# Differential attention on one core: two-bank score tiles, one softmax maximum per component, normalisation moved to the output

## The chip, the core and the metric

The kernel runs on one core of one Trainium2 chip. It is one program for a whole inference step. The metric is the device time of one execution in microseconds (us). Each engine (PE = TensorE, with its weight loads as PEld; DVE = VectorE; ACT = ScalarE; POOL = GpSimd; SP, which here only issues DMAs) works through its own list of instructions in a fixed order and waits at an instruction until its operands and its output buffer are ready.

## The reference, cut to what matters

The step has two layers. The second one's mixer is differential attention, for a prompt of 1024 tokens and for 8 sample sequences of 8 tokens. The change touches the prompt part, and one buffer of the sample part.

```
def diff_attend(q, q_pos, kv, k_pos, lam):            # 8 heads, 2 components of 64, values of 128
    s = einsum('bthcd,bshcd->bhcts', q * 64**-0.5, k)
    s = where(k_pos <= q_pos, s, NEG)
    a = softmax(s, axis=-1)
    w = a[:, :, 0] - lam * a[:, :, 1]
    return einsum('bhts,bshe->bthe', w, v)
def diff_out(o, ...):                                 # rms_norm over the 128 values of a head, then w_out
    return (rms_norm(o, subnorm) * (1 - lam_init)).reshape(B, T, -1) @ w_out
```

Each head has two score matrices (components). Each is softmaxed by itself, the second is subtracted with the factor lam, and the difference multiplies the values.

## The kernel before, in words

**Tiling.** The prompt's attention is cut into 64 units: 8 heads by 8 blocks of 128 queries. Unit (h, i) looks at the w = (i+1)*128 keys up to its own block. Units with i < 4 (w up to 512) are called short, the others long.

**A unit has two parts.** `scores(h, i)`, lines 1235 to 1275: for each component and for each stretch of up to 512 keys ("bank") PE computes the scores into a PSUM tile `S` of one bank (three of them, `SB`). DVE takes the negated row maximum (L1254), ACT takes exp with this maximum and sums the row (L1255) into the SBUF tile `P` (four of 128x1024, `PB`). A long unit has two banks per component with a maximum each, so DVE and ACT then bring the two to a common maximum with small operations on `ml` (L1259 to L1263, ACT's in L1261). DVE takes the reciprocals of the two sums (L1264) and multiplies them by 1 and -lam (L1265; for long units also L1267). POOL scales component 0 (L1271) and DVE adds component 1 times its factor (L1272), one bank at a time. `values(h, i)`, lines 1277 to 1297: PE transposes the weights in groups of four blocks into a PSUM tile `tr`, ACT copies them to `WT`, and PE multiplies them by V into a PSUM tile `av` of its own pool (two of them, `AVB`, shared with the sample's). DVE copies `av` to the output (L1294) and ACT sums its squares (L1296).

**PSUM.** There are 8 banks: three `S`, three `tr` (`TRB`), two `av`. The tile `tr` also serves the transposes of the sample's cached keys (`kt`, evicted to `KT` by DVE L99 and ACT L97 in turn), of the next head's keys and queries (`kn`, read by ACT and DVE in `qk_prep`), the sample's scores (`Qz`, L1388) and the transposes of a finished head (`fin`, L1300 to L1311).

**What sets the order.** The pieces of all units are Python generators. `stagger` merges them by a table of start times and durations: units of a head in the order 7, 0, 6, 1, 5, 2, 4, 3, each `values` behind its `scores` by `PLAG`, the sample's work spread over the same time. A list scheduler then fixes every engine's order when the program is built: it goes by that order and by its own estimate of when operands and buffers come free. Nothing is reordered on the chip.

**What follows.** `out_proj` (L770 to L815) multiplies the heads' outputs `oT` by w_out. It first splits them into two parts: `oh` by ACT (L97) and the rest by DVE and POOL (L104). Its first matmuls are `dn`. Head 7's `fin` runs inside it, on the PSUM tile `up`.

Of the kernel before, what the change touches and what calls it, by code (L numbers as in the profile page):

```python
# [12 lines left out]
AF = mybir.ActivationFunctionType  # L13
# [11 lines left out]
TRB, SB, AVB, KTB, KTT, VTB, VLAG, WTB, PLAG, PB, SEND = 3, 3, 2, 6, 4, 4, 5, 4, 6, 4, 0.92  # L25
# [46 lines left out]
class Step:  # L72
# [1114 lines left out]
    def diff_prompt(self, oT):  # L1187
# [3 lines left out]
        fac = kp("fac", [128, 2])  # L1191
# [10 lines left out]
        def begin():  # L1202
            self.diff_lambda(kp, sp)
            nc.vector.memset(fac[:, 0:1], 1.0)
            nc.vector.tensor_copy(fac[:, 1:2], self.nlam)
            yield
# [29 lines left out]
        def scores(h, i):  # L1236
# [4 lines left out]
            ml = sp("ml", [128, 14], bufs=3)  # L1241
            nm, l = (ml[:, x:x + 4].rearrange("p (n c) -> p n c", c=2) for x in (0, 4))
            banks = [(b0, min(w, b0 + 512)) for b0 in range(0, w, 512)]
            P = []
            for c in range(2):
                P.append(sp("P", [128, 1024], bufs=PB))
                for n, (b0, b1) in enumerate(banks):
                    S = pp("S", [128, 512], bufs=SB)
                    o = S[:, 0:b1 - b0]
                    self.mm(o, X[c][:, qs], A[c][:, b0:b1], True, False)  # L1250
                    self.mm(o, X[c][:, qs], B[c][:, b0:b1], False, b1 < w)
                    if b1 == w:
                        self.mm(S[:, w - 128 - b0:w - b0], self.identb, self.masks[:, 0, :], False, True)
                    nc.vector.tensor_reduce(nm[:, n, c:c + 1], o, AX.X, OP.max, negate=True)  # L1254
                    nc.scalar.activation(P[c][:, b0:b1], o, AF.Exp, bias=nm[:, n, c:c + 1], accum_out=l[:, n, c:c + 1])  # L1255
                    yield
            if len(banks) == 2:
                m, e = ml[:, 8:10], ml[:, 10:14].rearrange("p (n c) -> p n c", c=2)
                nc.vector.tensor_tensor(m, nm[:, 0], nm[:, 1], OP.min)  # L1259
                nc.vector.tensor_tensor(e, m.unsqueeze(1).to_broadcast([128, 2, 2]), nm, OP.subtract)  # L1260
                nc.scalar.activation(e, e, AF.Exp)  # L1261
                nc.vector.tensor_tensor(l, l, e, OP.mult)
                nc.vector.tensor_tensor(l[:, 0], l[:, 0], l[:, 1], OP.add)  # L1263
            nc.vector.reciprocal(l[:, 0], l[:, 0])  # L1264
            nc.vector.tensor_tensor(l[:, 0], l[:, 0], fac, OP.mult)  # L1265
            if len(banks) == 2:
                nc.vector.tensor_tensor(e, e, l[:, 0:1].to_broadcast([128, 2, 2]), OP.mult)  # L1267
            else:
                e = l
            for n, (b0, b1) in enumerate(banks):  # L1270
                nc.gpsimd.tensor_scalar(P[0][:, b0:b1], P[0][:, b0:b1], e[:, n, 0:1], 0.0, op0=OP.mult, op1=OP.add)  # L1271
                nc.vector.scalar_tensor_tensor(P[0][:, b0:b1], P[1][:, b0:b1], e[:, n, 1:2], P[0][:, b0:b1],  # L1272
                                               op0=OP.mult, op1=OP.add)
            st[h, i] = P[0]
            yield

        def values(h, i):
            V, ssq = st[h][3:]
            W = st[h, i]
# [9 lines left out]
            av = pp("av", [128, 128], bufs=AVB)  # L1289
# [4 lines left out]
            nc.vector.tensor_copy(oT[h][:, i * 128:i * 128 + 128], av)  # L1294
            sq = sp("sq", [128, 128], bufs=2)
            nc.scalar.activation(sq, av, AF.Square, accum_out=ssq[:, i:i + 1])  # L1296
# [21 lines left out]
        for h in range(8):  # L1318
            if h < 7:
                gens.append((t + 2, 40, 8, prep(h + 1)))  # L1320
            for i in (7, 0, 6, 1, 5, 2, 4, 3):
                gens.append((t, i + 2, 3 if i < 4 else 5, scores(h, i)))
# [302 lines left out]
```

## Time and profile before

| | us |
|---|---|
| median of 3 runs (3436.47 to 3440.07) | 3436.64 |
| the profiled execution, its own time | 3439.05 |
| its span, first to last instruction | 3437.3 |
| second attention and its end, 2131 to 2556 of the span | 425 |
| of these, 2131 to 2500 / 2500 to 2556 | 369 / 56 |

Times within the span count from its first instruction. Busy times of engines overlap. A wait is put down to what came last. The stretch from 2131 us, where the in-projection has ended on PE, to 2556 us, where `out_proj` runs steadily, holds nearly all that the change touches: the rest of the program is the first layer before it, and the second MLP behind it. The sample's attention runs all through the stretch to about 2512 us, beside the prompt's.

### The profile page before, as it was taken

The numbers are of one execution on the slowest core, as the hardware profiler recorded it, in microseconds if no ns is written. First come the engines' busy times: TensorE is split into PE (matmuls) and PEld (weight loads), VectorE is DVE, ScalarE is ACT, GpSimd is POOL, SyncE is SP. The second block draws the span as 40 slices with busy tenths as digits, with TensorE's granted clock in tenths as the row PEclk, the third lists the DMA queues.
The fourth block names the chain that finished last, engine by engine and source line by source line (L and its number), as shares of the span: only waits on it lengthen the run. The fifth ranks groups of instructions, "written<-read, shape, count | busy, mean of one in ns | idle before, by whom it ended". The sixth has DMA issues, their size and how long they took to land.

```text
span 3437.3 us, 59207 instructions
## 1 busy us (share of the span) xinstructions
PE 3325.9 (97%) x22990; PEld 2879.1 (84%) x22990; DVE 1907.2 (55%) x4043; ACT 1199.5 (35%) x2912; POOL 748.2 (22%) x1034
## 2 busy tenths in 40 slices
PE   8989989999999999999999999999979999999998
PEld 7779768787789999999997877777769899999998
DVE  5345666667655544444447224888764554444545
ACT  5222466666642111111114122777743111111111
POOL 1232235545421100011005113222220110011102
PEclk9999999999999999999999999999989999999999
DMA  7233510000022111111104223677522111111111
GB/s 251 77 102 112 151 56 14 18 21 2 1 84 68 50 44 33 48 50 50 44 32 157 74 77 120 200 231 240 191 84 75 43 48 45 31 50 50 50 31 53
DMA packets 243083, 271.01 MB, mean 79 GB/s; under 512 B 28626, under 2 KB 191602, under 8 KB 242674
## 3 DMA queue, kind: packets, MB, share of 16 engines
q1 hardware_dynamic: 242802, 267.23, 24.6%
q8 instruction: 181, 2.97, 0.4%
q14 instruction: 100, 0.82, 0.1%
HBM read 229.81 MB, written 41.50 MB: 79 GB/s over the span
## 4 chain that ended last, share of the span: by engine, by line
PE 63%; DVE 5%; ACT 3%; issue 0%; DMA 0%; POOL 0%; SPq 0%; DVEq 0%; ACTq 0%; POOLq 0%
PE dn L107 27%; PE up L107 22%; PE ps L107 8%; PE tr L110 2%; PE av L107 2%; PE S L107 1%; ACT P L1255 1%; DVE P L1272 1%; DVE ml L1254 1%; PE tr L1388 1%; DVE oT L104 1%; DVE hl L260 0%; DVE KT L99 0%; DVE xT L1088 0%; ACT WT L97 0%
## 5 line engine op out<-in xcount | busy, mean ns | idle before, releaser
L1088 DVE TENSOR_TENSOR xT<-xT,dn 128x512 f32<-128x512 f32 (+2 forms) x768 | 404.2, 530 | 497.3 <-PE dn L107 496.4
L107 PE MATMUL dn<-xh,dh 128*128 128x512 f32 (+2 forms) x1536 | 504.5, 328 | 0.7 <-DVE xT L1088 0.7
L107 PE MATMUL up<-hh,uh 128*128 128x512 f32 (+2 forms) x1536 | 503.9, 328 | 1.2 <-DVE u L1064 1.2
L107 PE MATMUL dn<-xl,dh 128*128 128x512 f32 (+2 forms) x1536 | 504.6, 329 | 0.0
L107 PE MATMUL dn<-xh,dl 128*128 128x512 f32 (+2 forms) x1536 | 503.4, 328 | 0.0
L107 PE MATMUL up<-hh,ul 128*128 128x512 f32 (+2 forms) x1536 | 502.8, 327 | 0.0
L107 PE MATMUL up<-hl,uh 128*128 128x512 f32 (+2 forms) x1536 | 502.4, 327 | 0.0
L100 POOL TENSOR_SCALAR xh<-u 128x512 fp32r<-128x512 f32 (+2 forms) x192 | 142.8, 744 | 1309.5 <-PE dn L107 858.6
L1065 ACT ACTIVATE u<-u 128x512 f32<-128x512 f32 (+2 forms) x192 | 96.4, 502 | 829.4 <-DVE u L1064 827.4
L107 PEld LDWEIGHTS up<-hh,uh 128*128 128x128 f32 x1536 | 289.7, 189 | 25.1 <-DVE u L1064 1.8
L107 PEld LDWEIGHTS up<-hl,uh 128*128 128x128 f32 x1536 | 289.7, 189 | 22.3
L107 PEld LDWEIGHTS up<-hh,ul 128*128 128x128 f32 x1536 | 289.6, 189 | 22.3
L107 PEld LDWEIGHTS dn<-xh,dh 128*128 128x128 f32 x1536 | 289.5, 189 | 21.5 <-DVE xT L1088 1.1
L107 PEld LDWEIGHTS dn<-xh,dl 128*128 128x128 f32 x1536 | 289.2, 188 | 21.6
L107 PEld LDWEIGHTS dn<-xl,dh 128*128 128x128 f32 x1536 | 289.4, 188 | 19.8
L721 POOL TENSOR_SCALAR P<-P,ml,gates 128x64 f32<-128x64 f32 (+8 forms) x384 | 244.7, 653 | 257.2 <-DVE ml L718 205.5
L107 PE MATMUL ps<-wh,hh 128*128 128x512 f32 (+2 forms) x720 | 277.2, 386 | 3.7 <-ACT hh L97 2.7
L107 PE MATMUL ps<-wh,hl 128*128 128x512 f32 (+2 forms) x720 | 277.3, 385 | 0.7 <-DVE hl L104 0.4
L107 PE MATMUL ps<-wl,hh 128*128 128x512 f32 (+2 forms) x720 | 277.2, 385 | 0.1
L107 PE MATMUL S<-A,X 128*128 128x512 f32 (+7 forms) x608 | 252.8, 416 | 23.3 <-ACT P L1255 11.1
L110 PE MATMUL tr<-ident,P 128*128 128x128 f32 (+1 forms) x1584 | 240.8, 281 | 17.9 <-DVE P L1272 10.6
L714 ACT ACTIVATE P<-S,ml 128x64 f32<-128x64 f32 (+8 forms) x384 | 216.6, 572 | 101.3 <-DVE ml L711 66.0
(334 smaller groups left out, 6423.8 us busy)
## 6 DMA issues: line engine op xcount, KB each, us to landing
ur<-in_mlp_w_up_dram SPq DMA_DIRECT2D x64, 512.0 KB
dr<-in_mlp_w_down_dram SPq DMA_DIRECT2D x64, 512.0 KB
kt<-in_cache_diff_kv_dram SPq DMA_DIRECT2D x64, 512.0 KB
vt<-in_cache_diff_kv_dram SPq DMA_DIRECT2D x64, 512.0 KB
xT<-x_saved SPq DMA_DIRECT2D x16, 544.0 KB
zq<-ro SPq DMA_DIRECT2D x32, 256.0 KB
kv<-in_cache_nsa_sel_dram SPq DMA_DIRECT2D x64, 128.0 KB
nat<-in_cache_nsa_cmp_dram SPq DMA_DIRECT2D x96, 64.0 KB
```

The costliest lines, as they stand in the source:

```text
L100: return self.nc.gpsimd.tensor_scalar(out, x, 1.0, 0.0, op0=OP.mult, op1=OP.add)
L104: e.tensor_tensor(out, x, h.bitcast(F32), OP.subtract)
L107: self.nc.tensor.matmul(out, lhsT, rhs, start=start, stop=stop)
L110: return self.nc.tensor.transpose(out, x, self.ident[:n, :n])
L714: nc.scalar.activation(P[:, c:c + x.shape[1]], x, AF.Exp, bias=nm[:, br:br + 1], accum_out=l[:, br:br + 1])
L721: nc.gpsimd.tensor_scalar(P[:, c0:c1], P[:, c0:c1], l[:, br:br + 1], g[:, br:br + 1], op0=OP.mult, op1=OP.mult)
L1065: nc.scalar.activation(u[:, :w], u[:, :w], AF.Square)
L1088: nc.vector.tensor_tensor(x, x, ps[:, :w], OP.add)
L1254: nc.vector.tensor_reduce(nm[:, n, c:c + 1], o, AX.X, OP.max, negate=True)
L1255: nc.scalar.activation(P[c][:, b0:b1], o, AF.Exp, bias=nm[:, n, c:c + 1], accum_out=l[:, n, c:c + 1])
L1272: nc.vector.scalar_tensor_tensor(P[0][:, b0:b1], P[1][:, b0:b1], e[:, n, 1:2], P[0][:, b0:b1], op0=OP.mult, op1=OP.add)
L1388: x = nc.tensor.matmul(o[qs, 0:256], Q[:, h], KT[2 * par + h // 4][:, h % 4 // 2, :], start=par == 1, stop=g > 0 and par == 0)
```

## The change

- `S` becomes a tile of two banks (128x1024), two of them instead of three of one bank. A long unit's component fills one tile, and has one maximum (L1260) and one exp (L1261) over all its w keys. A short unit puts both components into the two halves of one tile: one maximum operation for both (L1265), two exps (L1267), both into one `P` tile.
- The operations that bring two banks to one maximum are gone, and with them the constants `fac`.
- The weights are no longer normalised. One small operation forms -lam*l0/l1 (L1271) and one DVE operation over all w keys adds component 1 times it to component 0 (L1272). POOL's scaling is gone.
- 1/l0 is multiplied in at the output: DVE's copy of `av` becomes a multiplication by it (L1293), and ACT's square takes it as scale (L1295).
- The prompt's `av` is now a `tr` tile, so three banks serve both. The sample's `av` has one bank of its own. `ml` has six buffers instead of three.
- The last head's units run 7, 6, 5, 4, 3, 2, 1, 0. Short units' `scores` have two pieces instead of three.

The diff, without the lines that only drop `fac`:

```diff
-TRB, SB, AVB, KTB, KTT, VTB, VLAG, WTB, PLAG, PB, SEND = 3, 3, 2, 6, 4, 4, 5, 4, 6, 4, 0.92
+TRB, SB, KTB, KTT, VTB, VLAG, WTB, PLAG, PB, SEND = 3, 2, 6, 4, 4, 5, 4, 6, 4, 0.92
...
-            ml = sp("ml", [128, 14], bufs=3)
-            nm, l = (ml[:, x:x + 4].rearrange("p (n c) -> p n c", c=2) for x in (0, 4))
-            banks = [(b0, min(w, b0 + 512)) for b0 in range(0, w, 512)]
+            ml = sp("ml", [128, 6], bufs=6)
+            nm, l, r = ml[:, 0:2], ml[:, 2:4], ml[:, 4:6]
             P = []
+            S = None
             for c in range(2):
-                P.append(sp("P", [128, 1024], bufs=PB))
-                for n, (b0, b1) in enumerate(banks):
-                    S = pp("S", [128, 512], bufs=SB)
-                    o = S[:, 0:b1 - b0]
+
+                if c == 0 or w > 512:
+                    S = pp("S", [128, 1024], bufs=SB)
+                    P.append(sp("P", [128, 1024], bufs=PB))
+                else:
+                    P.append(P[0][:, 512:1024])
+                s0 = c * 512 if w <= 512 else 0
+                for b0 in range(0, w, 512):
+                    b1 = min(w, b0 + 512)
+                    o = S[:, s0 + b0:s0 + b1]
                     self.mm(o, X[c][:, qs], A[c][:, b0:b1], True, False)
                     self.mm(o, X[c][:, qs], B[c][:, b0:b1], False, b1 < w)
                     if b1 == w:
-                        self.mm(S[:, w - 128 - b0:w - b0], self.identb, self.masks[:, 0, :], False, True)
-                    nc.vector.tensor_reduce(nm[:, n, c:c + 1], o, AX.X, OP.max, negate=True)
-                    nc.scalar.activation(P[c][:, b0:b1], o, AF.Exp, bias=nm[:, n, c:c + 1], accum_out=l[:, n, c:c + 1])
+                        self.mm(S[:, s0 + w - 128:s0 + w], self.identb, self.masks[:, 0, :], False, True)
+                    if b1 < w:
+                        yield
+                if w > 512:
+                    nc.vector.tensor_reduce(nm[:, c:c + 1], S[:, 0:w], AX.X, OP.max, negate=True)
+                    nc.scalar.activation(P[c][:, 0:w], S[:, 0:w], AF.Exp, bias=nm[:, c:c + 1], accum_out=l[:, c:c + 1])
                     yield
-            if len(banks) == 2:
-                m, e = ml[:, 8:10], ml[:, 10:14].rearrange("p (n c) -> p n c", c=2)
-                nc.vector.tensor_tensor(m, nm[:, 0], nm[:, 1], OP.min)
-                nc.vector.tensor_tensor(e, m.unsqueeze(1).to_broadcast([128, 2, 2]), nm, OP.subtract)
-                nc.scalar.activation(e, e, AF.Exp)
-                nc.vector.tensor_tensor(l, l, e, OP.mult)
-                nc.vector.tensor_tensor(l[:, 0], l[:, 0], l[:, 1], OP.add)
-            nc.vector.reciprocal(l[:, 0], l[:, 0])
-            nc.vector.tensor_tensor(l[:, 0], l[:, 0], fac, OP.mult)
...
-            for n, (b0, b1) in enumerate(banks):
-                nc.gpsimd.tensor_scalar(P[0][:, b0:b1], P[0][:, b0:b1], e[:, n, 0:1], 0.0, op0=OP.mult, op1=OP.add)
-                nc.vector.scalar_tensor_tensor(P[0][:, b0:b1], P[1][:, b0:b1], e[:, n, 1:2], P[0][:, b0:b1],
-                                               op0=OP.mult, op1=OP.add)
-            st[h, i] = P[0]
+            if w <= 512:
+                Sv = S.rearrange("p (c k) -> p c k", c=2)[:, :, 0:w]
+                nc.vector.tensor_reduce(nm, Sv, AX.X, OP.max, negate=True)
+                for c in range(2):
+                    nc.scalar.activation(P[c][:, 0:w], Sv[:, c], AF.Exp, bias=nm[:, c:c + 1], accum_out=l[:, c:c + 1])
+                yield
+
+            nc.vector.reciprocal(r, l)
+            nc.vector.scalar_tensor_tensor(nm[:, 1:2], r[:, 1:2], self.nlam, l[:, 0:1], op0=OP.mult, op1=OP.mult)
+            nc.vector.scalar_tensor_tensor(P[0][:, 0:w], P[1][:, 0:w], nm[:, 1:2], P[0][:, 0:w], op0=OP.mult, op1=OP.add)
+            st[h, i] = P[0], r
             yield
...
-            av = pp("av", [128, 128], bufs=AVB)
+            av = tr()[:, 0:128]
...
-            nc.vector.tensor_copy(oT[h][:, i * 128:i * 128 + 128], av)
+            nc.vector.tensor_scalar(oT[h][:, i * 128:i * 128 + 128], av, r[:, 0:1], None, op0=OP.mult)
             sq = sp("sq", [128, 128], bufs=2)
-            nc.scalar.activation(sq, av, AF.Square, accum_out=ssq[:, i:i + 1])
+            nc.scalar.activation(sq, av, AF.Square, scale=r[:, 0:1], accum_out=ssq[:, i:i + 1])
...
-            for i in (7, 0, 6, 1, 5, 2, 4, 3):
-                gens.append((t, i + 2, 3 if i < 4 else 5, scores(h, i)))
+            for i in (7, 0, 6, 1, 5, 2, 4, 3) if h < 7 else (7, 6, 5, 4, 3, 2, 1, 0):
+                gens.append((t, i + 2, 2 if i < 4 else 5, scores(h, i)))
...
-                    self.av_s = pp("av", [128, 256], bufs=AVB)
+                    self.av_s = pp("av", [128, 512], bufs=1)[:, 0:256]
```

How the change moves instructions shows at two places. The first is PE's list in the middle of the attention, the same spot of the sample's work before and after: `tr<-ident,P` and the rows with `V` are of one unit's values, `kn` is the next head's key preparation, `kt` the sample's keys. On PE before:

```order
L110 MATMUL tr_25237<-ident_65,P_24963 128x128 x4
L110 MATMUL tr_25251<-ident_65,kn_24559 128x128 x4
L110 MATMUL tr_25263<-ident_65,kt_25258 128x128
L110 MATMUL tr_25263<-ident_65,kt_25259 128x128
L110 MATMUL tr_25263<-ident_65,kt_25258 128x128
L110 MATMUL tr_25263<-ident_65,kt_25259 128x128
L110 MATMUL tr_25269<-ident_65,P_24963 128x128 x2
L107 MATMUL av_25280<-V_23650,WT_25242 128x128 x4
L110 MATMUL tr_25292<-ident_65,kt_25258 128x128
L110 MATMUL tr_25292<-ident_65,kt_25259 128x128
L110 MATMUL tr_25292<-ident_65,kt_25258 128x128
L110 MATMUL tr_25292<-ident_65,kt_25259 128x128
```

On PE now, at the same spot:

```order
L110 MATMUL tr_25036<-ident_65,P_24776 128x128 x4
L110 MATMUL tr_25048<-ident_65,kn_24497 128x128 x4
L110 MATMUL tr_25055<-ident_65,P_24776 128x128 x2
L110 MATMUL tr_25066<-ident_65,kt_25025 128x128
L110 MATMUL tr_25066<-ident_65,kt_25026 128x128
L110 MATMUL tr_25066<-ident_65,kt_25025 128x128
L110 MATMUL tr_25066<-ident_65,kt_25026 128x128
L107 MATMUL tr_25072<-V_23587,WT_25041 128x128 x4
L107 MATMUL tr_25072<-V_23587,WT_25058 128x128 x2
L107 MATMUL S_25264<-A_24493,X_24491 128x512
L107 MATMUL S_25264<-B10_22724,X_24491 128x512
L107 MATMUL S_25264<-A_24493,X_24491 128x512
```

Five `tr` tiles now start one behind the other in three banks, where there were four and an `av` bank between them, and two banks of scores follow without a break.

The second is DVE's list at the end of the attention. `L104 ... oT<-oT,oh` are the splits for `out_proj`, `L1272` the combining of weights, `L1294` (now L1293) the copy of a unit's output. On DVE before:

```order
L104 TENSOR_TENSOR oT_29718<-oT_22688,oh_29717 128x512
L104 TENSOR_TENSOR oT_29718<-oT_22688,oh_29717 128x320
L1267 TENSOR_TENSOR ml_29531<-ml_29531 128x4
L104 TENSOR_TENSOR oT_29726<-oT_22689,oh_29725 128x512
L104 TENSOR_TENSOR oT_29726<-oT_22689,oh_29725 128x320
L1272 SCALAR_TENSOR_TENSOR P_29597<-P_29604,ml_29596,P_29597 128x512
L104 TENSOR_TENSOR oT_29829<-oT_22690,oh_29828 128x512
L104 TENSOR_TENSOR oT_29829<-oT_22690,oh_29828 128x320
L1272 SCALAR_TENSOR_TENSOR P_29532<-P_29554,ml_29531,P_29532 128x512
L1272 SCALAR_TENSOR_TENSOR P_29532<-P_29554,ml_29531,P_29532 128x128
L1294 COPY oT_22691<-av_29626 128x128
L1294 COPY oT_22691<-av_29642 128x128
```

On DVE now, at the end of the last head:

```order
L1272 SCALAR_TENSOR_TENSOR P_28970<-P_28970,ml_28968 128x256
L104 TENSOR_TENSOR oT_29107<-oT_22688,oh_29106 128x320
L1293 TENSOR_SCALAR oT_22691<-tr_28901,ml_28742 128x128
L104 TENSOR_TENSOR oT_29115<-oT_22689,oh_29114 128x512
L104 TENSOR_TENSOR oT_29115<-oT_22689,oh_29114 128x320
L104 TENSOR_TENSOR oT_29218<-oT_22690,oh_29217 128x512
L104 TENSOR_TENSOR oT_29218<-oT_22690,oh_29217 128x320
L1270 RECIPROCAL ml_28991<-ml_28991 128x2
L1271 SCALAR_TENSOR_TENSOR ml_28991<-ml_28991,nlam_22790 128x1
L1272 SCALAR_TENSOR_TENSOR P_28993<-P_28993,ml_28991 128x128
L1293 TENSOR_SCALAR oT_22691<-tr_28949,ml_28861 128x128
L1293 TENSOR_SCALAR oT_22691<-tr_28980,ml_28906 128x128
```

Before, the last two units to be combined were those with 512 and 640 keys, behind nearly all splits. Now only the units with 128 and 256 keys stand that late.

## Rows read from the trace of the kernel before

**Rows 1.** Windows: busy us of each engine (count), granted clock, DMA share, GB/s.

```profile
core 0: us, PE busy (x) PEld busy (x) DVE busy (x) ACT busy (x) POOL busy (x), PEclk, DMA share, GB/s
2131.00:2180.00 49.00, 41.43 (x335) 33.27 (x334) 40.01 (x104) 33.66 (x99) 13.48 (x29) 0.90 0.76 247
...
2131.00:2500.00 369.00, 343.37 (x3275) 272.20 (x3274) 306.08 (x862) 271.73 (x809) 96.35 (x163) 0.98 0.68 220
2500.00:2556.00 56.00, 32.80 (x160) 27.61 (x159) 36.59 (x101) 27.43 (x79) 18.71 (x20) 0.70 0.27 90
```

**Rows 2.** PE's waits, 2180 to 2500: line waited for, total us, times, longest.

```profile
PE S L107 <- ACT P L1255: 3.2, 7, 0.8
PE tr L110 <- DVE KT L99: 2.6, 5, 1.0
...
PE tr L110 <- ACT WT L97: 2.1, 4, 0.7
```

**Rows 3.** Waits of all engines, 2100 to 2560.

```profile
POOL P L1271 <- DVE ml L1267: 77.3, 18, 7.8
...
ACT P L1255 <- DVE P L1272: 21.5, 22, 4.7
...
ACT sq L1296 <- DVE oT L1294: 11.6, 11, 3.3
...
DVE P L1272 <- POOL P L1271: 11.2, 18, 0.9
```

**Rows 4.** DVE's groups by shape, 2100 to 2560: busy us, mean ns, idle before.

```profile
L1254 DVE TENSOR_REDUCE ml<-S 128x1 f32<-128x512 f32 x96 | 64.8, 684 | 8.2 <-PE S L107 7.6
...
L1272 DVE SCALAR_TENSOR_TENSOR P<-P,ml 128x512 f32<-128x512 f32 x48 | 41.4, 870 | 8.9 <-POOL P L1271 8.3
...
L1265 DVE TENSOR_TENSOR ml<-ml,fac 128x2 f32<-128x2 f32 x64 | 11.6, 184 | 1.0
...
L1254 DVE TENSOR_REDUCE ml<-S 128x1 f32<-128x128 f32 x32 | 9.1, 283 | 1.5 <-PE S L107 1.5
...
L1272 DVE SCALAR_TENSOR_TENSOR P<-P,ml 128x128 f32<-128x128 f32 x16 | 5.5, 343 | 1.0 <-POOL P L1271 0.8
...
L1263 DVE TENSOR_TENSOR ml<-ml 128x2 f32<-128x2 f32 x32 | 5.0, 157 | 0.5
```

**Rows 5.** ACT's groups by shape, 2100 to 2560.

```profile
L1255 ACT ACTIVATE P<-S,ml 128x512 f32<-128x512 f32 x96 | 65.8, 689 | 21.1 <-DVE P L1272 10.3 <-DVE ml L1254 7.6 <-DVE ml L1259 1.9
...
L1255 ACT ACTIVATION_READ_ACCUMULATOR P<-S,ml 128x1 f32 x192 | 39.3, 205 | 0.0
...
L1255 ACT ACTIVATE P<-S,ml 128x128 f32<-128x128 f32 x32 | 11.8, 368 | 6.4 <-DVE P L1272 4.4 <-DVE ml L1254 2.0
...
L1261 ACT ACTIVATE ml<-ml 128x4 f32<-128x4 f32 x32 | 6.9, 216 | 3.6 <-DVE ml L1260 3.5
```

**Rows 6.** Groups by line with shapes merged, 2131 to 2556: PE's av, POOL's scaling.

```profile
L107 PE MATMUL av<-V,WT 128*128 128x128 f32 x576 | 82.7, 285 | 3.0 <-DVE ao L1429 1.0 <-ACT sq L1296 0.9 <-ACT WT L97 0.9
...
L1271 POOL TENSOR_SCALAR P<-P,ml 128x512 f32<-128x512 f32 (+2 forms) x96 | 58.5, 618 | 222.3 <-DVE ml L1267 77.3 <-DVE ml L1265 38.9 <-PE S L107 20.4
```

**Rows 7.** PE's longest wait, 2500 to 2556.

```profile
PE tr L110 <- DVE P L1272: 10.6, 1, 10.6
```

**Rows 8.** Timeline of the end: start, us, engine, line, instruction.

```profile
2509.01 0.80 PE L107 MATMUL tr<-KT,ones 128*128 128x128 f32 x2 [1.56 <-DVE KT L1505]
...
2538.03 2.15 PE L110 MATMUL tr<-ident,P 128*128 128x128 f32 x9 [10.60 <-DVE P L1272]
...
2543.13 0.19 ACT L1296 ACTIVATION_READ_ACCUMULATOR sq<-av 128x1 f32 x1
```

**Rows 9.** ACT's groups by line with shapes merged, 2131 to 2556.

```profile
L97 ACT ACTIVATE WT<-tr 128x512 f32<-128x512 f32 (+2 forms) x96 | 46.2, 487 | 20.6 <-PE tr L110 20.0
...
L1296 ACT ACTIVATE sq<-av 128x128 f32<-128x128 f32 x64 | 17.8, 280 | 12.0 <-DVE oT L1294 11.6
...
L97 ACT ACTIVATE oh<-oT 128x512 fp32r<-128x512 f32 (+2 forms) x24 | 10.4, 508 | 0.1
```

More of the change, by code (lines that the diff above doesn't have):

```diff
@@ L1190, in diff_prompt @@
         kp, sp, pp = self.dp["late"], self.dp["prompt"], self.pp
-        fac = kp("fac", [128, 2])
         kv = io["o8"][0, 0].rearrange("(t p) e h d -> p t e h d", p=128)
@@ L1203, in begin @@
             self.diff_lambda(kp, sp)
-            nc.vector.memset(fac[:, 0:1], 1.0)
-            nc.vector.tensor_copy(fac[:, 1:2], self.nlam)
             yield
@@ L1264, in scores @@
-            nc.vector.reciprocal(l[:, 0], l[:, 0])
-            nc.vector.tensor_tensor(l[:, 0], l[:, 0], fac, OP.mult)
[L1266 to L1269, printed above, removed]
-            for n, (b0, b1) in enumerate(banks):
-                nc.gpsimd.tensor_scalar(P[0][:, b0:b1], P[0][:, b0:b1], e[:, n, 0:1], 0.0, op0=OP.mult, op1=OP.add)
-                nc.vector.scalar_tensor_tensor(P[0][:, b0:b1], P[1][:, b0:b1], e[:, n, 1:2], P[0][:, b0:b1],
-                                               op0=OP.mult, op1=OP.add)
@@ L1278, in values @@
             V, ssq = st[h][3:]
-            W = st[h, i]
+            W, r = st[h, i]
             WT = []
```

## The prediction, made before the result was known

> **What bounds the kernel now.** I read the windows first, to find which engine is full in which stretch, then the waits of that engine, then the groups by shape for the price of each operation, then the timeline of the end. From 2131 to 2500 us PE is busy for 343.37 of 369 us, DVE for 306.08 and ACT for 271.73 [rows 1]. So the long middle of the attention is PE's, and what can be won there is at most PE's idle time, 369 - 343.37 = 25.6 us. Of it 49.00 - 41.43 = 7.6 us lie in the first 49 us, before the pipeline has filled. That leaves 18 us. PE's named waits after 2180 us are small and spread: 3.2 us for a score tile that ACT still reads, 2.6 and 2.1 us for transposes' banks that DVE and ACT still empty [rows 2]. The end, 2500 to 2556, is different: PE is busy for 32.80 of 56 us at a granted clock of 0.70, between its two levels of 1.2 and 2.4 GHz, after long idle stretches [rows 1], and one wait of 10.6 us for the combined weights of the last two units makes up nearly half of the idle time [rows 7].
>
> **Part by part.** The change adds and removes no matmul, so PE's own work is the same. What it takes from the others:
>
> DVE, maxima. A 128-column maximum takes 283 ns and a 512-column one 684 ns [rows 4], so 149 ns are fixed and a column costs 1.04 ns. The columns stay the same; 192 operations become 64 of long components and 32 of short units. That saves 96 x 0.149 = 14.3 us. No row shows widths over 512 or the form with two results. At worst a wide one costs as much as the two that it replaces (0 saved), at best the line above holds; I take the line, as two shapes of one operation fix it.
>
> DVE, combining. 343 ns at 128 columns and 870 at 512 [rows 4] give 167 ns fixed. 96 operations become 64: 5.3 us.
>
> DVE, small operations. L1259, L1260, L1262, L1263 and L1267 go: 5 x 32 x 0.157 = 25 us at the row of L1263; L1265's 184 ns become one of about 160 [rows 4], 1.5 us. The output copy becomes a multiplication by a column. Its price is between 0 and one more small operation, 64 x 0.157 = 10 us; I take 0, as it moves the same 128 columns. DVE in all: about 46 of 306.08 + 36.59 = 343 us [rows 1].
>
> ACT. An exp costs 368 ns at 128 and 689 ns at 512 columns, so 261 ns are fixed, and each sum is read out for 205 ns more [rows 5]. 192 become 128: 64 x 0.466 = 29.8 us, and L1261's 6.9 us go too. Together 36.7 of 271.73 + 27.43 = 299 us.
>
> POOL loses its scaling, 58.5 us [rows 6]. It was not full, but the weights went through it. It waited 77.3 us for DVE's small operations, DVE waited 11.2 us for POOL, and ACT's exps stood 21.5 us until the combination had freed a `P` tile [rows 3]. In ACT's list the evictions for PE stand behind such an exp. This chain of up to ten operations on three engines becomes three on DVE, and a short unit uses one `P` tile instead of two.
>
> None of this is on PE. It counts only as far as PE's 18 us are waits for late evictions. Bounds: 0 (other waits take their place) and -18. I take half, -9, since DVE and ACT lose about an eighth each and ACT's 21.5 us of standing go.
>
> Score tiles. A two-bank tile is held after its last matmul for maximum, exp and sum: for the mean long width of 832 columns 1.02 + 0.96 + 0.205 = 2.2 us by the lines above, for a short unit (mean 320 columns per component) about 2.3 us. 96 such tiles in two places give 96 x 2.2 / 2 = 106 us; before, 192 tiles of mean 384 columns at 1.3 us in three places gave 83 us. The wait of 3.2 us [rows 2] stands behind this. Between none and its double I take no change, since the room is 369 us.
>
> Transpose banks. The prompt's `av` now takes one of the three `tr` banks. It holds it for its matmuls, 82.7 / 64 = 1.3 us [rows 6], and for ACT's square with its sum, 0.28 + 0.205 us [rows 9, 5], some 1.8 us, 64 times: 114 us of bank time. Bounds: 0, and 114 / 3 = 38 us if every bit of it holds PE up. PE's list shows the tightening: five tiles in a row where there were four and a separate `av`. As transposes' banks cost PE only 2.6 and 2.1 us now [rows 2], I take a value near the lower end, +6.
>
> ACT's square waits for DVE's copy of the same tile, 11.6 us in 11 cases [rows 3]: the two readers come one after the other. The Trainium skill ("PSUM — Partial Sum Buffer", section "PSUM bank collisions raise a hardware error") states that two engines must not be in one bank and partition quadrant at a time, readers included; the trace agrees. By that rule a `tr` bank that holds an `av` is shut for both readers in turn, and this change puts 64 such tiles into the banks that PE needs most. By the rule the time would go to that of the slower rival below, by [rows 2] alone the +6 would be nearer to 0.
>
> The end. From the last product of the sample's norm at 2509.01 to the last square of head 7 at 2543.13 + 0.19 there are 34.3 us [rows 8]. In them PE waits 10.6 us for the combined weights of units 3 and 4 [rows 7], which stand behind `out_proj`'s splits on DVE. Now the last units are 1 and 0, with 256 and 128 columns, and what sets the pace is ACT's list. From the same point on it holds 21 splits x 0.508 = 10.7, 10 copies of transposed weights x 0.487 = 4.9, 7 squares x 0.485 = 3.4 [rows 9, 5], 6 exps of 384, 256 and 128 columns at about 0.68 with their sums = 4.1, and 2 evictions of head 6 at about 0.69 by the 512-column exp = 1.4 [rows 5]: 24.5 us. For the way through PE and back I add 3 us; it is between 0 and another wait like the one of 10.6. So 27.5 instead of 34.3: -7, between -10 and +1. Everything behind the last square stays as it is.
>
> Sum: -9 + 6 - 7 = -10 us. The profiled execution took 3439.05 us (span 3437.3), so 3429 of its kind; it lies 2.4 us above the median of 3436.64, on which I forecast 3427.
>
> **Rivals.** *Slower: the transpose banks.* Place: PE before a `tr` tile, in the middle. Half of the 38 us falls on PE, 19, and the lighter DVE and ACT give nothing, because the bank and not the queue is late; the end still gives 7. +12: about 3449. It decides from 16 us of added bank waits on, where it has eaten the other two terms. For it: the tight list, and the readers in turn [rows 3]. Against it: waits for these banks are small now, and DVE and ACT, which empty them, have less queued.
>
> *Faster: PE runs freely.* All 18 us of the middle go, the banks cost nothing, the end gives 10: -28, 3409. For it: ACT's 21.5 us and POOL's 77.3 us [rows 3] show that latency, not work, delays the weights. Against it: some waits hang on transfers and on the order itself.
>
> *No change.* In the middle the two terms cancel, and at the end DVE's splits again stand ahead of what PE needs, since the order is written beforehand. 3437. For it: PE is 93% busy in the middle. Against it: the last units are really shorter.
>
> **How the numbers follow.** A measurement here can tell about 0.2%, 7 us, from no change. Forecast 0.42, by itself 3419 to 3433, with 0.04 of it within 0.2%; free PE 0.14; no change 0.18; banks 0.26. Faster 0.38 + 0.14 = 0.52, same 0.04 + 0.18 = 0.22, slower 0.26. The range reaches from a little below the free PE, 3407, to the price of the banks, 3449, and leaves out the far ends of both, 2 in 10.
>
> **What would show it.** In the changed profile DVE's busy time from 2131 us to the end of the attention should be near 297 us, ACT's near 262, POOL's near 56. PE's waits for a `P` or `WT` in the last 50 us should be under 5 us, and the way from the sample's last norm product to the last square near 27 us. PE's waits before `tr` tiles on DVE's and ACT's readers of `av` (L1293, L1295) and of `KT` and `WT` tell the forecast (some 10 us) from the slower rival (over 20). It is wrong if the middle, up to the sample's end, becomes longer by more than the end becomes shorter, or if the score tiles' wait grows to several times 3.2 us.

## The result and the profile after

The changed kernel takes 3468.61 us (median of 6 runs, 3466.84 to 3471.11), the kernel before beside it on the same chip 3439.77 (3436.47 to 3441.7): 1.0086 times the time, with a 95% interval of 1.0073 to 1.0099. It is slower by 29 us, and outside the predicted range. The page of the changed kernel's profiled execution (3471.11 us):

```profile
span 3469.3 us, 58579 instructions
...
PE 3336.5 (96%) x22990; PEld 2879.2 (83%) x22990; DVE 1879.1 (54%) x3753; ACT 1186.6 (34%) x2752; POOL 687.2 (20%) x938
```

PE issues the same 22990 matmuls as before. The first place to look is the point at which the sample's norm product starts on PE: 2509.01 before [rows 8], 2544.96 now. So the middle is 36 us longer, and the way from there to the last square 4.3 us shorter (the timeline below). I compare the middle up to this point, first for the kernel before (columns as in [rows 1]):

```profile
2131.00:2509.00 378.00, 348.96 (x3300) 276.03 (x3298) 314.26 (x894) 276.50 (x822) 99.06 (x168) 0.97 0.69 224
2131.00:2556.00 425.00, 376.18 (x3433) 299.80 (x3432) 342.67 (x962) 299.17 (x886) 115.06 (x182) 0.94 0.63 203
```

and for the changed kernel, with the stretch of [rows 1] ahead:

```profile
2131.00:2500.00 369.00, 325.03 (x2971) 251.50 (x2973) 257.08 (x537) 237.34 (x595) 38.27 (x72) 0.98 0.64 205
...
2131.00:2545.00 414.00, 362.18 (x3298) 278.91 (x3296) 288.49 (x616) 262.99 (x660) 41.53 (x76) 0.98 0.64 206
...
2131.00:2588.00 457.00, 391.72 (x3433) 304.36 (x3432) 313.02 (x673) 287.17 (x726) 54.94 (x86) 0.95 0.59 189
```

The first two columns behind the length tell most. In the same 369 us PE now gets through 2971 matmuls where there were 3275. For the same 3300 matmuls it needs 414 us in place of 378, at a granted clock of 0.98 and 0.97, so the clock is not the reason. Its idle time grows from 378.00 - 348.96 = 29.0 to 414.00 - 362.18 = 51.8 us, and its "busy" time by 13.2 us for the same work. So a part of the stalls stands inside the busy time: the weight loads of the same work, PEld, took 276.03 and 278.91 us, all but the same, and a transpose of `kt` takes 280 ns in both; the matmuls only overlap less. The Trainium skill ("Perfetto Trace Analysis", section "Identifying the Most-Contended Engine") says that the busy time of matmuls is not a good measure of how close PE is to its limit, because they are pipelined, and names that of weight loads as one to use instead. This trace agrees. One profile places the marker to some 5 us only: a second execution of the changed kernel (e15) has it at 2540.0, with PE busy for 356.75 us at a clock of 0.99. The other engines are less busy, as forecast, and PE does not profit.

PE's waits up to the same point, for the kernel before (line waited for, total us, times, longest):

```profile
PE S L107 <- ACT P L1255: 7.0, 11, 1.7
PE tr L110 <- DVE Ps L1421: 2.9, 4, 1.4
...
PE tr L1388 <- ACT KT L97: 1.8, 3, 0.8
...
PE tr L110 <- ACT KT L97: 1.4, 3, 0.7
```

and for the changed kernel:

```profile
PE S L107 <- ACT P L1261: 8.2, 16, 2.0
PE tr L1387 <- ACT KT L97: 6.2, 9, 0.9
PE S L107 <- ACT P L1267: 5.9, 5, 2.7
PE tr L110 <- DVE KT L99: 5.5, 10, 0.8
PE tr L110 <- ACT KT L97: 5.2, 9, 0.7
PE tr L110 <- ACT WT L97: 3.3, 9, 1.0
...
PE tr L107 <- ACT WT L97: 1.7, 6, 0.4
...
PE tr L110 <- ACT sq L1295: 1.6, 3, 0.6
```

No single row is large. Summed over all rows in which a `tr` tile waits for ACT, DVE or POOL (for its bank or its operand), without the marker's own wait, there are 12.4 us in 22 waits before and 28.9 us in 55 now. Before, the prompt's products wait on rows that name `av`, 2.8 us in 7 cases, which this sum leaves out. It is what I follow through the experiments; for the score tiles the waits are 7.0 and 14.1 us. All rows together make up 26.6 of PE's 29.0 us of idle time before, and 48.4 of its 51.8 now.

The groups that answer to [rows 4, 5, 9], 2100 to 2590 us:

```profile
L1295 ACT ACTIVATE sq<-tr,ml 128x128 f32<-128x128 f32 x64 | 23.3, 368 | 12.2 <-DVE oT L1293 12.0
...
L1293 DVE TENSOR_SCALAR oT<-tr,ml 128x128 f32<-128x128 f32 x64 | 22.2, 347 | 10.5 <-PE tr L107 10.2
...
L1260 DVE TENSOR_REDUCE ml<-S 128x1 f32<-128x1024 f32 x16 | 19.5, 1223 | 3.0 <-PE S L107 2.8
...
L1261 ACT ACTIVATE P<-S,ml 128x1024 f32<-128x1024 f32 x16 | 17.8, 1112 | 5.0 <-DVE ml L1260 4.8
...
L1271 DVE SCALAR_TENSOR_TENSOR ml<-ml,nlam 128x1 f32<-128x1 f32 x64 | 15.4, 241 | 1.5
...
L1265 DVE TENSOR_REDUCE ml<-S 128x2 f32<-128x1024 f32 x8 | 9.8, 1224 | 0.8
...
L1272 DVE SCALAR_TENSOR_TENSOR P<-P,ml 128x512 f32<-128x512 f32 x8 | 6.0, 752 | 0.2
```

A maximum over 1024 columns takes 1223 ns and an exp 1112 ns; the prediction's lines give 1214 and 1117. The multiplication of the output takes 347 ns against the copy's 282, and the square 368 against 280 [rows 9]: each of the 64 `av` holds its bank longer by about 0.15 us.

How long an `av` holds its bank in all shows in the timeline. One unit of the changed kernel, from its first product to the readout of its square's sum:

```profile
2464.34 0.89 PE L107 MATMUL tr<-V,WT 128*128 128x128 f32 x6
...
2465.79 0.35 DVE L1293 TENSOR_SCALAR oT<-tr,ml 128x128 f32<-128x128 f32 x1
...
2467.28 0.37 ACT L1295 ACTIVATE sq<-tr,ml 128x128 f32<-128x128 f32 x1
...
2467.53 0.21 ACT L1295 ACTIVATION_READ_ACCUMULATOR sq<-tr,ml 128x1 f32 x1
```

The tile stays for 3.40 us, and for half of that nobody works on it: first DVE is still at its maxima of scores, then ACT at an exp of 1024 columns. Taken over all 64 units, in order of time, the mean is 3.67 us, 235 us in all. The kernel before, whose `av` have banks of their own, has 3.98 us, 255 in all; one of its units, with 3.30 us:

```profile
2352.63 1.95 PE L107 MATMUL av<-V,WT 128*128 128x128 f32 x16
...
2354.82 0.28 DVE L1294 COPY oT<-av 128x128 f32<-128x128 f32 x1
...
2355.57 0.26 ACT L1296 ACTIVATE sq<-av 128x128 f32<-128x128 f32 x1
...
2355.73 0.20 ACT L1296 ACTIVATION_READ_ACCUMULATOR sq<-av 128x1 f32 x1
```

The end, on PE and ACT (start, us, engine, line, instruction):

```profile
2544.96 0.79 PE L107 MATMUL tr<-KT,ones 128*128 128x128 f32 x2 [1.71 <-DVE KT L1504]
...
2557.32 2.93 PE L107 MATMUL tr<-V,WT 128*128 128x128 f32 x12 [4.04 <-ACT WT L97]
...
2563.92 2.08 PE L107 MATMUL tr<-V,WT 128*128 128x128 f32 x8 [2.60 <-ACT WT L97]
...
2574.82 0.19 ACT L1295 ACTIVATION_READ_ACCUMULATOR sq<-tr,ml 128x1 f32 x1
```

The wait of 10.6 us [rows 7] is gone. In its place PE waits for `WT` in ACT's list, 4.04 and 2.60 us at the longest, 8.7 us in all, as its waits from 2545 to 2576 us show:

```profile
PE tr L107 <- ACT WT L97: 8.7, 7, 4.0
```

From the norm product to the last square there are 30.05 us where there were 34.3.

### The profile page after: what moved, and what is told of

Its sections match the earlier page's. It is cut to its first block, busy times and chain, and to the rows that moved or that the text cites. A ratio compares the mean times of both kernels' runs of the same rounds, so it can differ in the third digit from the quotient of the medians.

```text
span 3469.3 us, 58579 instructions
## 1 busy us (share of the span) xinstructions
PE 3336.5 (96%) x22990; PEld 2879.2 (83%) x22990; DVE 1879.1 (54%) x3753; ACT 1186.6 (34%) x2752; POOL 687.2 (20%) x938
## 4 chain that ended last, share of the span: by engine, by line
PE 64%; DVE 4%; ACT 3%; issue 1%; DMA 0%; POOL 0%; DVEq 0%; SPq 0%; ACTq 0%
PE dn L107 26%; PE up L107 22%; PE ps L107 8%; PE tr L110 2%; PE S L107 2%; PE tr L107 2%; PE tr L1387 1%; PE av L107 1%; ACT P L1261 1%; ACT WT L97 1%; DVE hl L260 0%; DVE P L1272 0%; ACT KT L97 0%; DVE xT L1088 0%; DVE oT L104 0%
## 5 line engine op out<-in xcount | busy, mean ns | idle before, releaser
L107 PEld LDWEIGHTS dn<-xh,dh 128*128 128x128 f32 x1536 | 289.5, 188 | 21.5 <-DVE xT L1088 1.0
```

The costliest lines, as they stand in the source:

```text
L107: self.nc.tensor.matmul(out, lhsT, rhs, start=start, stop=stop)
```

## The experiments

Two theories stood against each other. *Banks*: the prompt's `av` in the three transpose banks holds PE up. *Others*: the two-bank score tiles, the weights' new chain or the new order do. Each run was timed beside the kernel before. "Norm product at" is where that marker stands in the profiled execution, and "`tr` waits" is the sum named above, up to it. The list scheduler knows the banks and the pieces, so every edit also brings another written order; e11 and e13 to e16 show what an order alone does.

| run | median us (range) | ratio, 95% interval | norm product at | `tr` waits, us (times) |
|---|---|---|---|---|
| before | 3439.77 | 1 | 2509.0 | 12.4 (22) |
| changed | 3468.61 | 1.0073 to 1.0099 | 2545.0 | 28.9 (55) |
| e1 | 3460.54 (3459.13 to 3462.33) | 1.0047 to 1.0081 | 2531.5 | 25.2 (53) |
| e2 | 3434.9 (3430.16 to 3438.68) | 0.9978 to 0.9997 | 2509.4 | 12.2 (27) |
| e3 | 3437.4 (3430.95 to 3440.88) | 0.998 to 0.9999 | 2511.6 | 11.3 (25) |
| e4 | 3435.5 (3433.45 to 3439.21) | 0.9979 to 0.9999 | 2508.3 | 12.9 (27) |
| e5 | 3466.26 (3463.28 to 3470.23) | 1.0061 to 1.0094 | 2537.4 | 21.4 (47) |
| e6 | 3457.34 (3454.61 to 3460.47) | 1.0037 to 1.007 | 2530.1 | 29.2 (51) |
| e7 | 3440.06 (3434.3 to 3445.36) | 0.9988 to 1.0007 | 2513.0 | 15.0 (29) |
| e8 | 3433.64 (3430.34 to 3438.84) | 0.9974 to 0.9993 | 2509.2 | 13.8 (26) |
| e9 | 3492.35 (3490.34 to 3499.58) | 1.0141 to 1.0175 | 2560.5 | 37.7 (72) |
| e10 | 3460.78 (3457.3 to 3463.57) | 1.0042 to 1.0076 | 2537.8 | 25.5 (49) |
| e11 | 3433.3 (3427.64 to 3443.0) | 0.9971 to 0.9992 | 2505.0 | 12.9 (24) |
| e12 | 3430.91 (3426.55 to 3436.11) | 0.9969 to 0.9989 | 2499.3 | 10.6 (18) |
| e13 | 3463.85 (3462.13 to 3465.34) | 1.0054 to 1.0092 | 2540.7 | 25.3 (56) |
| e14 | 3430.45 (3428.57 to 3436.12) | 0.9967 to 0.9986 | 2515.8 | 11.9 (28) |
| e15 (changed, again) | 3465.87 (3464.75 to 3469.9) | 1.0065 to 1.0104 | 2540.0 | 29.0 (55) |
| e16 | 3425.67 (3422.89 to 3427.28) | 0.9951 to 0.9974 | 2505.3 | 12.6 (26) |

The kernel before took 3439.23 beside e1 to e4, 3441.09 beside e5 to e8, 3439.53 beside e9 to e12 and 3437.95 beside e13 to e16.

**e1: the sharing alone, in the kernel before.**

```diff
-            av = pp("av", [128, 128], bufs=AVB)
+            av = tr()[:, 0:128]
...
-                    self.av_s = pp("av", [128, 256], bufs=AVB)
+                    self.av_s = pp("av", [128, 512], bufs=1)[:, 0:256]
```

> The kernel before with one part of the change alone: the prompt's av is a tile of the three transpose banks, and the sample's av has one bank of its own. Score tiles, weights and the order of the last head stay as before. Theory A (banks): the 36 us that the changed kernel loses in the middle come from av in the transpose banks; this kernel then takes 3460 to 3475 us, and PE's waits before tr tiles between 2180 and 2500 us rise from about 11 to over 20 us. Theory B (score tiles): they come from score tiles of two banks, two deep, with maxima and exps up to 1024 columns wide; this kernel then stays within 3430 to 3446 us.

It costs 21.3 us (3460.54 - 3439.23). Its middle, columns as in [rows 1]:

```profile
2131.00:2531.50 400.50, 361.11 (x3298) 276.90 (x3298) 313.40 (x891) 279.33 (x822) 96.73 (x165) 0.98 0.65 212
```

DVE, ACT and POOL do what they did before (314.26, 276.50 and 99.06 us); only the same 3298 matmuls take 22.5 us more. PE's waits there, the longest rows on `tr` tiles:

```profile
PE tr L1388 <- ACT KT L97: 4.2, 8, 0.7
PE tr L107 <- ACT WT L97: 3.3, 8, 1.0
PE tr L110 <- ACT WT L97: 3.0, 8, 0.8
```

PE waits more often, not longer, and mostly for the transposes' own evictions. That fits an `av` in the ring making the tiles behind it late; rows that name `sq` have only 1.4 us. An `av` holds its bank for 3.24 us here, 208 us in all, read as above.

**e2: the same with a fourth transpose bank**, which e1 leaves unused.

```diff
-TRB, SB, AVB, KTB, KTT, VTB, VLAG, WTB, PLAG, PB, SEND = 3, 3, 2, 6, 4, 4, 5, 4, 6, 4, 0.92
+TRB, SB, AVB, KTB, KTT, VTB, VLAG, WTB, PLAG, PB, SEND = 4, 3, 2, 6, 4, 4, 5, 4, 6, 4, 0.92
```

> As the first kernel of this call, but with four transpose banks instead of three (three score banks, four transpose banks, one for the sample's av: all eight). Theory A: the fourth bank gives most of the loss of the three-bank kernel back, 3435 to 3450 us. Theory B: nothing was lost there, so both lie within 5 us of each other and of the kernel before.

All of it comes back, 25.6 us. PE's middle is that of the kernel before again:

```profile
2131.00:2509.35 378.35, 349.17 (x3307) 278.07 (x3306) 311.69 (x893) 276.50 (x823) 99.09 (x167) 0.98 0.69 225
```

**e3: the weights' part alone, in the kernel before**: common maximum ahead of the exps, one combining operation, no scaling on POOL, 1/l0 at the output; PSUM and the last head as before.

```diff
+                if len(banks) == 2:
+                    nc.vector.tensor_tensor(nm[:, 0, c:c + 1], nm[:, 0, c:c + 1], nm[:, 1, c:c + 1], OP.min)
+                for n, (b0, b1) in enumerate(banks):
+                    nc.scalar.activation(P[c][:, b0:b1], os[n], AF.Exp, bias=nm[:, 0, c:c + 1], accum_out=l[:, n, c:c + 1])
...
+            nc.vector.reciprocal(r, l[:, 0])
+            nc.vector.scalar_tensor_tensor(nm[:, 0, 1:2], r[:, 1:2], self.nlam, l[:, 0, 0:1], op0=OP.mult, op1=OP.mult)
+            nc.vector.scalar_tensor_tensor(P[0][:, 0:w], P[1][:, 0:w], nm[:, 0, 1:2], P[0][:, 0:w], op0=OP.mult, op1=OP.add)
```

> The kernel before with the weights part alone: PSUM stays as before (three one-bank score tiles, av in its own two banks), a long unit takes two maxima, their minimum, and two exps with the common maximum; the combination in one DVE operation, no POOL, 1/l0 at the output; last head in the old order. Theory A: the loss is in the banks, so this kernel is faster than before by what the shorter chain gives, 3420 to 3436 us. Theory B: the same, since the wide score tiles are not in it, too. A third theory, that a common maximum or the longer combination itself delays PE, expects 3445 us or more.

1.8 us faster, at the edge of what can be told from nothing and 1.4 us above the range of the first two theories, although POOL's busy time in the middle falls from 99.06 to 45.78 us and DVE's from 314.26 to 296.18. So no gain shows from the shorter chain that another order could not bring as well (e11).

**e4: the last head's units long to short, in the kernel before.**

```diff
-            for i in (7, 0, 6, 1, 5, 2, 4, 3):
+            for i in (7, 0, 6, 1, 5, 2, 4, 3) if h < 7 else (7, 6, 5, 4, 3, 2, 1, 0):
```

> The kernel before with only the last head's units in the order 7 to 0. By the prediction's term for the end: 3 to 7 us faster, 3431 to 3437 us, the way from the sample's last norm product to the last square shorter than 34.3 us. Rival: the order that the scheduler writes puts the splits ahead of what PE needs again, and the time stays within 3437 to 3445 us.

3.7 us faster. The way from the norm product to the last square is 30.65 us against 34.3, about what the changed kernel has (30.05). But e11, which leaves this order alone, has 29.35 us with a wait of 10.8 us for the combined weights still in it, so the shortening can't be given to the edit.

**e5: the changed kernel with one-bank score tiles** (three of them, with the exps of e3).

```diff
-TRB, SB, KTB, KTT, VTB, VLAG, WTB, PLAG, PB, SEND = 3, 2, 6, 4, 4, 5, 4, 6, 4, 0.92
+TRB, SB, AVB, KTB, KTT, VTB, VLAG, WTB, PLAG, PB, SEND = 3, 3, 2, 6, 4, 4, 5, 4, 6, 4, 0.92
...
-                    S = pp("S", [128, 1024], bufs=SB)
+                    S = pp("S", [128, 512], bufs=SB)
```

> The changed kernel with the score tiles of before: three of one bank each, two maxima and their minimum per long component, an exp per bank. av stays in the three transpose banks, weights and last head are as changed. If the rest of the loss (about 36 us in the middle less the 22 that av in the transpose banks cost alone) is the two-bank score tiles', this takes 3450 to 3458 us. If the score tiles cost nothing and the parts make each other worse once the banks are short, it takes 3464 us or more.

The loss stays: 25.2 us against 28.8, and the two intervals overlap. In the middle the marker comes 7.5 us earlier, of which two executions of one kernel can differ by 5 (e15), and 3.7 are lost at the end (33.8 us from the norm product to the last square). By themselves the two-bank tiles cost little or nothing.

**e6: the changed kernel, the square read from SBUF**, so that a `tr` bank with an `av` has one reader.

```diff
-            nc.scalar.activation(sq, av, AF.Square, scale=r[:, 0:1], accum_out=ssq[:, i:i + 1])
+            nc.scalar.activation(sq, oT[h][:, i * 128:i * 128 + 128], AF.Square, accum_out=ssq[:, i:i + 1])
```

> The changed kernel with one edit: ACT squares the scaled output in SBUF instead of the tile in PSUM, so a transpose bank that holds av is free after DVE's copy alone, about 0.55 us earlier. If the length of the hold is what PE pays for, 64 times up to 0.55 us = up to 35 us of bank time less, 3450 to 3462 us. If what counts is that one more kind of tile takes a bank at all, and in which order, it stays within 3463 to 3472 us.

Some 12 us come back: the loss against the kernel before is 16.3 us in place of 28.8. The square itself also becomes cheaper, as its rows show beside the changed kernel's 368 ns:

```profile
L1295 ACT ACTIVATE sq<-oT 128x128 f32<-128x128 f32 x64 | 19.6, 309 | 13.1 <-DVE oT L1293 10.8 <-DVE rs_t L118 1.6 <-DVE P L1272 0.5
```

The bank is free when DVE's copy ends, 2.27 us after the first product in place of 3.67 us to the readout (145 us in all in place of 235). This run alone does not part the shorter hold of the bank from ACT's lighter list.

**e7: four transpose banks, one-bank scores, weights' part, new order of the last head. e8: the same with the square from SBUF.** The edits are those of e2, e3, e4 and, for e8, e6.

> A version meant to beat both kernels: one-bank score tiles (three), four transpose banks that also take the prompt's av, one bank for the sample's; weights and last head as in the change. If the gains measured one by one add up (4 us for the four banks, 2 for the weights, 4 for the last head), 3426 to 3432 us. If the last head's order and the weights gain the same waits, 3432 to 3437 us.

> The previous kernel of this call with ACT's square from SBUF. If the hold of a bank still costs with four of them, 2 to 6 us faster than that kernel. If four banks are enough, within 2 us of it.

With four banks nothing of the loss is left, though the weights' part and the new order of the last head are in. But e7 is not faster than the kernel before, 3 us over the higher of its two ranges: the gains measured one by one do not add up. The square from SBUF gives 6.4 us even with four banks; the two intervals touch, and an order alone can move as much (e11). So how e6's 12 us are shared between the bank and ACT's list stays open.

**e9: the kernel before with two transpose banks** (`TRB` 2, nothing else): what one bank less costs.

> The kernel before with two transpose banks instead of three, nothing else. If the changed kernel's loss is a shortage of transpose banks, taking a whole bank away costs more than sharing one did (22 us in the middle): 3470 us or more, most of it before the sample's last norm product, with PE's waits before tr tiles the longest of all. If PE is bound by its own work and the banks hardly matter, within 3436 to 3450 us.

It costs 52.8 us. The middle, and the longest of PE's waits before `tr` tiles:

```profile
2131.00:2560.50 429.50, 369.78 (x3306) 279.41 (x3304) 320.81 (x894) 281.63 (x823) 96.93 (x168) 0.97 0.61 198
```

```profile
PE tr L110 <- ACT WT L97: 9.1, 20, 1.5
PE tr L110 <- ACT KT L97: 5.1, 10, 0.7
PE tr L110 <- DVE KT L99: 4.9, 9, 1.4
```

If a part of a bank costs its share of these 52.8 us, which was not tried by itself, the sharing can be estimated. The prediction's bank time of 114 us is 114 / 378 = 0.30 of a bank over the middle: 16 us, too little. The bank time that the traces show, 208 of 400.5 us in e1 and 235 of 414 in the changed kernel, gives 27 and 30 us against 21.3 and 28.8 measured. For e6, 145 of 399 us, it gives 19 against 16.3, for e10 below, 243 of 407 us, 32 against 21.3. So the estimate holds to some 10 us here.

**e10: the changed kernel with the last head in its old order.**

```diff
-            for i in (7, 0, 6, 1, 5, 2, 4, 3) if h < 7 else (7, 6, 5, 4, 3, 2, 1, 0):
+            for i in (7, 0, 6, 1, 5, 2, 4, 3):
```

> The changed kernel with the last head's units in the old order (7, 0, 6, 1, 5, 2, 4, 3). If the new order is worth the same 4 us here as on the kernel before, 3470 to 3475 us. If it has made the middle longer, because the last head's long units come in a row and each takes two score tiles of two banks, faster than the changed kernel: 3455 to 3465 us.

It is faster than the changed kernel by about 8 us: the order that went with a gain of 3.7 us in e4 goes with a loss here. Both are near what an order alone does (e11). Its loss against the kernel before, 21.3 us, is that of e1.

**e11: the kernel before, one number of the planner changed** (`SEND` 0.93 for 0.92), with the same instructions in another written order.

> The kernel before with one number of the table changed that moves no work between engines: the sample's work is spread over 0.93 of the prompt's time instead of 0.92. It shows how far the time moves when only the written order is another one. If orders of the same quality lie within 5 us, 3434 to 3445 us, and effects of 2 to 5 us in the other runs are not to be given to an edit. If it moves by more than 10 us, the 22 us of av in the transpose banks could be such a draw, too.

6.2 us faster, a little below the range. So a difference of up to some 6 us between two orders tells nothing about the edit that brought them, and the gains of e3 and e4 can't be given to their edits.

**e12: e8 with the old order of the last head.**

> The fastest version so far (four transpose banks with av, one-bank scores, weights as changed, square from SBUF) with the last head in the old order. If the new order is worth 4 us here, 3436 to 3440 us; if the end no longer hangs on it, since the weights come sooner, within 2 us of 3434.

8.6 us faster than the kernel before, 0.9978 of its time, and 3 us under e8: in neither range, and no more than an order's difference.

**e13, e14 and e16: the same questions in the other written order** (`SEND` 0.93): e1's sharing, e2's fourth bank, and e12. **e15** was meant to be the changed kernel in that order, but its kernel is the changed kernel as it was, with `SEND` at 0.92; the third text below does not describe it.

> The kernel before with the prompt's products in the three transpose banks, under the planner's 0.93 in place of 0.92. Banks: the loss against 0.93 without the sharing (3433.3) stays, 15 to 25 us, so 3448 to 3458. Written order: the loss falls under 8 us, 3433 to 3441.

> As the run before, with four transpose banks, under 0.93. Banks: the fourth bank gives the loss back under this order too, 3427 to 3437, at least 12 us under the run before. Written order: no more than 5 us between the two.

> The changed kernel under 0.93 with nothing else altered. Banks: it stays 15 us or more above the kernel before, 3455 to 3472. Written order: within 8 us of the kernel before, 3432 to 3448.

> Four transpose banks with the prompt's products in them, one-bank scores, the weights' part, the square from SBUF, the last head in its old order, under 0.93: 3430.9 under 0.92. Either theory: 3424 to 3437; it is the fastest only if the two gains of 6 to 9 us add, 3424 to 3428.

The loss belongs to the banks, in either order: with the sharing 3463.85, 6 us over its range and some 30 above e11; with a fourth bank 3430.45, 33.4 us apart. Their middles, e13:

```profile
2131.00:2540.70 409.70, 367.50 (x3330) 280.26 (x3329) 317.35 (x902) 280.76 (x829) 99.58 (x174) 0.97 0.64 209
```

and e14:

```profile
2131.00:2515.75 384.75, 357.15 (x3333) 283.85 (x3332) 312.62 (x902) 278.32 (x829) 101.30 (x175) 0.97 0.68 222
```

e15 repeats the changed kernel: 3465.87 us, 1.0085 of the time before, where the first measurement had 1.0086. It says how far two profiles of one kernel differ, here in the middle:

```profile
2131.00:2540.00 409.00, 356.75 (x3295) 275.25 (x3293) 287.67 (x615) 262.62 (x660) 40.86 (x76) 0.99 0.65 208
```

The changed kernel under 0.93 was not run. e16 beats both kernels: 3425.67 us, 0.9962 of the time before, and 40 us under e15 beside it. It keeps the change's weights and gives the transposes the bank that two-bank scores had taken.

The four pairs that differ in `SEND` alone (the kernel before and e11, e1 and e13, e2 and e14, e12 and e16) lie 6.2, 4.6, 3.2 and 3.7 us apart, each run taken against the kernel before beside it. That is the size of an order's effect; the banks' 21 to 33 us are more than three times the largest of them.

## Why the prediction was wrong

**The step that failed is "I take a value near the lower end, +6" for the transpose banks, and the bank time under it.** Alone the sharing measures 21.3 us in one written order (e1) and some 30 in the other (e13 against e11), and against a fourth bank 25.6 and 33.4 us (e1 against e2, e13 against e14). Two readings led to +6.

The first is of [rows 2]: waits of 2.6 and 2.1 us were to show slack. They don't: e9 shows that the third bank, at whose side those small waits stand, is worth 52.8 us. A small wait says how late the last bank is now, not how late it will be with a little less of it. Nor are these two rows all: in the same window the rows in which a `tr` tile waits for ACT or DVE sum to 10.4 us.

The second is the hold of 1.8 us, 114 us in all. It adds up the products, the square and its readout. It leaves out DVE's copy of 0.28 us, although the next paragraph says that the readers come one after the other, and the time in which the tile stands before either reader. The trace of the kernel before has 3.98 us, 255 in all, and with the sharing it is 208 (e1) and 235 us (changed kernel). So the upper bound of 38 us was too low as well. By e9's price 114 us lead to 16 us, and even with that the sum would have been 0 and not +29; 208 us lead to 27.

**"-9" for the lighter DVE and ACT did not show.** e3 has the lighter engines without the sharing, and gains 1.8 us, less than a mere other order can give; e7 has them with four banks, and gains nothing. The 77.3 and 21.5 us of POOL's and ACT's waits [rows 3] were for the most part waits off PE's path. The frame of this term was wrong too: "at most PE's idle time, 25.6 us" took PE's busy time for work, and 8 to 13 us of the middle's loss stand inside it.

**The engines' work fell less than forecast.** From 2131 us to the steady `out_proj` DVE's busy time is 313.02 us (forecast near 297), ACT's 287.17 (near 262), POOL's 54.94 (near 56). By groups ACT lost 31.6 us: exps 110.7 to 93.9, readouts 39.3 to 25.9, L1261's 6.9, and the squares gained 5.5. But its busy time fell only 299.17 - 287.17 = 12.0 us. Durations of neighbours on one engine overlap, so a sum over groups overstates what an engine gets back, and a readout of 205 ns is the extreme case: from 2131 to 2556 us before, ACT's 264 readouts last 54.1 us in all, and its busy time without them would be 7.8 us less. The same holds for DVE: 44 us by the groups, 29.7 in the windows, although the small operation of L1271 took 241 ns where about 160 were put. No gain in time from this shows.

**The score tiles, "no change"**: right within what can be told (e5). PE's waits for them doubled, 7.0 to 14.1 us, the upper bound that the step named, but one-bank tiles give back only some 2 us of the total.

**The end, "-7"**: the wait of 10.6 us went, but the way became only 4.3 us shorter (34.3 to 30.05), because PE's waits for `WT` came in its place, 8.7 us over the end where the prediction asked for under 5. That it became shorter is luck as far as the new order goes: with the old order the way is 29.1 us in e10 and 29.35 in e11.

**The slower rival** named the place and the mechanism, the count of `tr` waits over 20 us included (28.9). Its 3449 was still too low: it subtracted an end of 7 us, and took half of a bank time that was itself too small. Of the 29 us, some 21 go with the sharing as e1 has it; the other 7 to 8 go away with the old order of the last head (e10). Which edit they belong to stays open, since orders alone move the time by up to 6 us (e11).

## What to carry to other kernels

Price a tile that moves into a shared PSUM ring by its bank time, and not by how small the ring's waits are now. Read the hold from the timeline, from the first write to the end of the last reader: here the sum of the operations alone was half of it. The share of a bank that this makes, times what a whole bank is worth when one is taken away, came within some 10 us here. Count PE's matmuls, or the busy time of their weight loads, in a stretch: its own busy time hides stalls. Where a planner writes the order, change one of its numbers alone first, to see how much an order by itself moves the time.

## What the runs showed of the hardware that was not expected

- **A column as operand has a price.** The output's copy became a multiplication by a column, 282 to 347 ns for 128 columns (the operation changed with it), and the square with the column as scale went from 280 to 368 ns. I had taken 0 for the first and had not priced the second. The Trainium skill ("ScalarE: Activation LUTs", section "What ACT_TABLE_LOAD costs") gives about 93 ns for each such operand of an ACT instruction; the 88 ns measured here agree.
- **DVE's combining became cheaper where POOL's scaling is gone**: 870 to 752 ns at 512 columns, the same operation [rows 4]. At 128 columns it is 343 and 350 ns. It is not that both components now lie in one `P` tile: e3 keeps them in two and has 745 ns. Whether POOL's scaling slowed it was not tried by itself.
- **Stalls can show as busy time on PE**: the same 3300 matmuls were busy for 348.96, 361.11, 362.18 and 369.78 us (before, e1, changed, e9) at granted clocks of 0.97 to 0.98, and for 356.75 us at 0.99 when the changed kernel ran again (e15).
